# K and V, and pairs of Q units, projected 512 columns at a time in a two-layer trunk

## Chip, cores and metric

The kernel runs on one core of one Trainium2 chip. The metric is the device time of one execution in microseconds (us). The engines of the core are named as the profile names them: PE is TensorE (matmuls; PEld its weight loads), DVE is VectorE, ACT is ScalarE, POOL is GpSimd, SP is SyncE, which mostly issues DMAs. Each engine works through its own instructions in program order and waits on semaphores for the others.

## What is computed

The reference is a trunk of two layers over 512 tokens of width 1024 (fp32). Layer 0 mixes by pooling; layer 1 is sliding-window attention with sink logits over K and V that are computed once, from the stream after layer 0. Each layer ends with a convolutional GLU of width 2816.

```python
D_MODEL = 1024; SEQ = 512; D_FF = 2816
HEAD_DIM = 64; N_Q_HEADS = 16; N_KV_HEADS = 4; WINDOW = 128
# layer 0
x = x + rms_norm(pool_mixer(rms_norm(x, g)), g_post)
x = x + rms_norm(conv_glu_ffn(rms_norm(x, g)), g_post)
# shared K and V
kv = (rms_norm(x, kv_norm_g) @ w_kv).reshape(B, S, 2, 4, 64)
k, v = rope(kv[:, :, 0]), kv[:, :, 1]
# layer 1
q = rope((rms_norm(x, g) @ w_q).reshape(B, S, 16, 64))
m = swa_sink_attention(q, banded(k), banded(v), sinks) @ w_o
x = x + rms_norm(m, g_post)
x = x + rms_norm(conv_glu_ffn(rms_norm(x, g)), g_post)
```

In the attention, a block of 128 queries sees its own block of 128 keys and the one before it, with a causal window of 128; the sink logit of a head enters the maximum and the sum of its softmax only.

## The kernel before

Every large product is computed from fp32 operands that are split into a high and a low fp32r part: high x high, low x high and high x low (`mm3`, lines 318, 319 and 320). So each weight goes through a load from HBM (`raw`), a cast on ACT that makes the high part `wh`, and a subtraction on DVE that makes the low part `wl`. A weight **unit** is 128 x 2048 numbers. `split(i)` makes `wh` and `wl` of unit i in a slot (three slots, or a buffer of its own named in `homes`) and starts the loads of the next two; `ahead` keeps the splits three units in front of the products.

The instructions of PE, ACT, DVE and POOL run in the order in which the program is written; there is no scheduler. In time order the stages are:

- the pooling mixer of layer 0, to about 46 us of the span;
- FFN0's up products. Each of the 22 iterations j of the loop in `first` takes 48 matmuls of 512 columns (`up`), the convolution on ACT and DVE (`act`: lines 535 to 551), sums of the weights for the down product on POOL at even j (`w_sums`), sums of the gated values on POOL at odd j (`g_sums`), and `ahead`. `split1` splits gated values (lines 575, 577, 578);
- FFN0's down products, `pass1` from 289 us and `pass2` to 399 us;
- the projections of K and V, and then the attention with Q's projections, to about 560 us;
- layer 1's FFN, in the same way, to the end.

Six weight units of layer 1 are made ready early: `prepare(i, h)` reads half h of unit i in FFN0's loop, makes its high and low parts, and stores them to DRAM (`ready`). When such a unit is needed, `split` only loads both parts, by DMAs that ACT issues. Units of K, V and Q also get the gain of their normalisation in this place: four casts with a scale on ACT and four operations on DVE (line 174) instead of one and one (line 169). READY holds K, V, two of the four Q units, and two units of FFN1; the 12 halves are prepared at j = 3, 4, 6, 7, 9, 10, 12, 13, 15, 16, 18 and 19:

```python
if l == 0 and j >= 3 and j % 3 != 2 and j < 21:
    k = (j - 3) // 3 * 2 + j % 3
    prepare(READY[k // 2], k % 2)
```

The other two Q units go through `scale` (on POOL, line 183) and `piece` (lines 194 and 198) in the first eight attention steps.

K and V are projected block by block of 128 tokens, 256 columns at a time (`proj`, PSUM tiles `kp` and `vp`): blocks 2 and 3 first, then `to_attention` transposes blocks 0 and 1 of the normalised stream into `xTh_a` and `xTl_a`, with K's own transposes (`k_T`, tile `kt`) between, then blocks 0 and 1. `rotate` applies the rotary embedding (two products on DVE, two sums on POOL), and `kst` is its copy that PE transposes.

The attention has 16 steps, one for each of the four groups of heads g and the four blocks b, in the order of g and then b. Step i issues the scores of its own (g, b), normalises the softmax of step i - 1, transposes the probabilities of step i - 2 (`p_T`, tile `pT`; `PTl` is their low part), multiplies those of step i - 3 with V (`pv`), and projects Q of step i + 3 (`q_proj`, tile `qp`, 24 matmuls of 256 columns). `q_rot`, `q_parts`, `q_low` and `q_T` rotate Q, split it (`qst`) and transpose it (`qt`, then `qT`). The table `todo` spreads Q's and the output projection's weight pieces over the steps. The normalisation is a reciprocal and four products, three on DVE and one on POOL:

```python
for h in range(4):
    eng = nc.gpsimd if h == 3 else nc.vector
    eng.tensor_scalar(Pt[:, h, 0:w], Pt[:, h, 0:w], dn[:, h : h + 1], None, ALU.mult)
```

## Time and profile before

| | |
|---|---|
| three runs | 929.82, 930.46, 934.66 us (median 930.46) |
| the profiled execution | 935.51 us, of which the span is 933.7 us |
| PE, DVE, ACT, POOL busy | 98%, 70%, 50%, 35% of the span |
| mean granted PE clock | 0.99 |
| matmul and other PE instructions | 4702 |

The span runs from the first to the last instruction that the profiler shows. A row of the waits gives who waits at which line for whom, the total in us, how often, and the longest. A row of a timeline gives start and duration in us, engine, line, operation, what it writes and reads with the shape, and how many like it were put together; in brackets stands the idle time before it and what ended that. A row of the groups gives line, engine, operation, tiles, shapes and count, then the busy time in us and the mean in ns, then the idle time in front. Matmuls overlap, so the distance between two starts is their pace, not their duration.

### The profile page before, as it was taken

The page shows a single profiled execution, that of the slowest core. Times are in us where ns is not written, and L with a number is a line of the kernel's source. Part 1 is how long each engine was busy: PE and PEld are TensorE (multiplying, and loading weights), DVE is VectorE, ACT ScalarE, POOL GpSimd, SP SyncE. Part 2 cuts the span into 40 slices and gives each one's busy share as a digit, 9 for nine tenths or more (in the row PEclk, how much of TensorE's full clock was granted, in tenths as well). Part 3 has the DMA queues.
Part 4 walks back from the last instruction along what each step waited for, and adds up shares of the span by engine and source line. Part 5 has one row for each costly group of instructions (what it writes and reads, how often), then busy time and mean ns, then how long its engine had stood idle before and what let it go on. Part 6 is the DMA issues. An engine that isn't in the chain of part 4 may idle for free.

```text
span 933.7 us, 12782 instructions
## 1 busy us (share of the span) xinstructions
PE 912.5 (98%) x4702; PEld 781.0 (84%) x4702; DVE 654.2 (70%) x948; ACT 466.7 (50%) x815; POOL 324.0 (35%) x381
## 2 busy tenths in 40 slices
PE   8999999999999999999999999999999999999996
PEld 7898888888887878799899888988888888888785
DVE  4787867867577777953999836565555565677877
ACT  4734544444445565653688734433334433455562
POOL 1644434444442000234656403244444433410001
PEclk7999999999999999999999999999999999999999
DMA  8263888887884665732112144445554555456642
GB/s 307 91 227 114 312 301 308 257 324 262 295 279 147 218 217 180 277 151 92 47 46 91 49 178 145 149 181 183 202 209 184 205 203 189 159 158 206 219 171 112
DMA packets 45040, 178.49 MB, mean 191 GB/s; under 512 B 5297, under 2 KB 6833, under 8 KB 36658
## 3 DMA queue, kind: packets, MB, share of 16 engines
q1 hardware_dynamic: 43250, 165.10, 50.6%
q10 hardware_dynamic: 1728, 12.58, 3.5%
q8 instruction: 37, 0.61, 0.3%
q14 instruction: 25, 0.20, 0.1%
HBM read 139.91 MB, written 37.75 MB: 190 GB/s over the span
## 4 chain that ended last, share of the span: by engine, by line
PE 79%; DVE 10%; issue 3%; POOL 3%; ACT 3%; DMA 2%; POOLq 0%; SPq 0%; DVEq 0%; ACTq 0%
PE u L319 16%; PE u L320 16%; PE u L318 16%; PE dn L319 5%; PE dn L320 5%; PE dn L318 5%; DVE wl L232 2%; DVE xn_f L303 1%; DVE P L907 1%; PE op L318 1%; PE op L319 1%; PE op L320 1%; PE qp L320 1%; PE qp L318 1%; PE qp L319 1%
## 5 line engine op out<-in xcount | busy, mean ns | idle before, releaser
L319 PE MATMUL u<-xTl_f,wh 128*128 128x512 f32 (+1 forms) x768 | 285.4, 372 | 2.0 <-DVE xTl_f L315 2.0
L318 PE MATMUL u<-xTh_f,wh 128*128 128x512 f32 (+1 forms) x768 | 285.7, 372 | 0.2 <-ACT xTh_f L314 0.2
L320 PE MATMUL u<-xTh_f,wl 128*128 128x512 f32 (+1 forms) x768 | 285.2, 371 | 0.0
L232 DVE TENSOR_TENSOR wl<-raw,wh 128x1024 fp32r<-128x1024 f32 (+1 forms) x158 | 205.8, 1343 | 13.6 <-ACT wh L231 13.3
L319 PEld LDWEIGHTS u<-xTl_f,wh 128*128 128x128 f32 x768 | 144.7, 188 | 27.5 <-DVE xTl_f L315 2.5
L536 DVE SCALAR_TENSOR_TENSOR t<-u,conv,t 128x511 f32<-128x511 f32 x88 | 65.8, 748 | 144.3 <-ACT t L535 144.3
L318 PEld LDWEIGHTS u<-xTh_f,wh 128*128 128x128 f32 x768 | 144.7, 188 | 25.1 <-ACT xTh_f L314 0.5
L320 PEld LDWEIGHTS u<-xTh_f,wl 128*128 128x128 f32 x768 | 144.7, 188 | 25.0
L231 ACT CAST wh<-raw 128x1024 fp32r<-128x1024 f32 (+1 forms) x158 | 156.8, 1040 | 9.2 <-DMA raw<-t 6.4
L535 ACT ACTIVATE t<-u,conv 128x512 f32<-128x512 f32 x88 | 68.2, 776 | 137.3 <-PE u L320 103.2
L556 POOL TENSOR_TENSOR G<-G,G 128x256 f32<-128x256 f32 x22 | 33.3, 1515 | 270.6 <-DVE G L551 270.6
L319 PE MATMUL dn<-wl,gh 128*128 128x512 f32 x276 | 108.0, 391 | 3.1 <-DVE wl L232 3.1
L320 PE MATMUL dn<-wh,gl 128*128 128x512 f32 x276 | 107.6, 390 | 0.1
L318 PE MATMUL dn<-wh,gh 128*128 128x512 f32 x276 | 107.6, 390 | 0.0
L544 ACT ACTIVATE t<-t 128x512 f32<-128x512 f32 x44 | 27.8, 633 | 104.4 <-DVE t L537 104.4
L537 DVE SCALAR_TENSOR_TENSOR t<-u,conv,t 128x510 f32<-128x510 f32 x88 | 65.9, 749 | 3.1
L319 PEld LDWEIGHTS dn<-wl,gh 128*128 128x128 f32 x276 | 51.8, 188 | 15.6 <-DVE wl L232 5.1
L320 PEld LDWEIGHTS dn<-wh,gl 128*128 128x128 f32 x276 | 51.8, 188 | 11.2 <-DVE gl L650 0.6
L318 PEld LDWEIGHTS dn<-wh,gh 128*128 128x128 f32 x276 | 51.8, 188 | 10.8
L252 POOL TENSOR_SCALAR ss_p_f<-ss_p_f 128x1 f32<-128x1 f32 x8 | 3.3, 417 | 159.5 <-ACT dn L250 159.5
L577 ACT CAST gh<-G 128x1024 fp32r<-128x1024 f32 x22 | 23.1, 1051 | 56.4 <-DVE G L575 44.1
L578 DVE TENSOR_TENSOR gl<-G,gh 128x1024 fp32r<-128x1024 f32 x22 | 27.5, 1250 | 26.6 <-ACT gh L577 21.0
(197 smaller groups left out, 1544.9 us busy)
## 6 DMA issues: line engine op xcount, KB each, us to landing
raw<-in_ws_dram SPq DMA_DIRECT2D x49, 1024.0 KB, 5.0
q<-in_ws_dram SPq DMA_DIRECT2D x44, 512.0 KB, 6.4
raw<-t SPq DMA_DIRECT2D x24, 768.0 KB, 5.6
t<-q SPq DMA_DIRECT2D x44, 256.0 KB, 2.9
t<-q SPq DMA_DIRECT2D x22, 512.0 KB, 2.8
raw<-in_ws_dram SPq DMA_DIRECT2D x22, 512.0 KB, 4.4
r<-in_ws_dram SPq DMA_DIRECT2D x12, 512.0 KB, 6.6
hi<-h SPq DMA_DIRECT2D x12, 512.0 KB, 6.4
```

The costliest lines, as they stand in the source:

```text
L231: nc.scalar.copy(hi[:, s], r[:, s])
L232: nc.vector.tensor_tensor(lo[:, s], r[:, s], hi[:, s].bitcast(F32), ALU.subtract)
L318: nc.tensor.matmul(acc, ah, bh, start=first, stop=False)
L319: nc.tensor.matmul(acc, ah, bl, start=False, stop=False)
L320: nc.tensor.matmul(acc, al, bh, start=False, stop=last)
L535: nc.scalar.activation(t, u, AF.Identity, bias=conv_col(l, ch, 3), scale=conv_col(l, ch, 2))
L536: nc.vector.scalar_tensor_tensor(t[:, 1:], u[:, : S - 1], conv_col(l, ch, 1), t[:, 1:], ALU.mult, ALU.add)
L537: nc.vector.scalar_tensor_tensor(t[:, 2:], u[:, : S - 2], conv_col(l, ch, 0), t[:, 2:], ALU.mult, ALU.add)
L544: nc.scalar.activation(tg, tg, AF.Gelu_apprx_tanh)
L556: nc.gpsimd.tensor_tensor(s1, s1, G2[:, p, 2, :], ALU.add)
L577: nc.scalar.copy(h, G1[:, o : o + 1024])
L578: nc.vector.tensor_tensor(lo, G1[:, o : o + 1024], h.bitcast(F32), ALU.subtract)
```

## The change

1. `proj` multiplies 512 columns at a time. K and V are taken together: `prepare` stores the halves of K's and V's units side by side, in 1 KB segments, so that one unit holds K and V for four of the eight k, and the second for the other four. The same is done with Q's units in pairs. A pair's projection takes 4 k from each of two units.
2. READY gets the last two Q units at its end, so all of Q is prepared in FFN0: 16 halves, at all j from 1 to 21 that are no multiple of 4. `scale` and Q's entries of `todo` go; the two units are loaded by ACT's DMAs when needed.
3. The softmax is normalised by one product on DVE over the four heads, with the reciprocal broadcast.
4. The steps run over pairs of groups: (2 pr + i, b) for pr, then b, then i. `q_rot`, `q_parts` and `q_low` work on 512 columns every second step; `q_proj(m, part)` gives one half of a pair's projection per step. The output projection's pieces are spread over steps 4 to 15. Buffers move: `kT` uses the tags `whk` and `wlk`, which a unit of FFN1 takes over; `rA`, `rB` and `st` have fewer and larger buffers; the last `o32` is in `rA`'s. `start1` and `ffn_start(1, ...)` now stand inside the scope of the attention's pool.

```diff
-READY = (U_K, U_V, U_Q, U_Q + 1, U_IN[1], U_IN[1] + 1)
+READY = (U_K, U_V, U_Q, U_Q + 1, U_IN[1], U_IN[1] + 1, U_Q + 2, U_Q + 3)
...
-        nc.sync.dma_start(ready[i][0][:, s], hi.bitcast(F32))
-        nc.sync.dma_start(ready[i][1][:, s], r)
+        if i >= U_IN[1]:
+            o = [t[:, s] for t in ready[i]]
+        else:
+            side = (i - U_K) % 2
+            o = [t.rearrange("p (k s c) -> p k s c", k=4, s=2)[:, :, side, :] for t in ready[i - side + h]]
+            hi, r = (t.rearrange("p (k c) -> p k c", k=4) for t in (hi, r))
+        nc.sync.dma_start(o[0], hi.bitcast(F32))
+        nc.sync.dma_start(o[1], r)
...
-            if l == 0 and j >= 3 and j % 3 != 2 and j < 21:
-                k = (j - 3) // 3 * 2 + j % 3
+            if l == 0 and j % 4:
+                k = j - 1 - j // 4
                 prepare(READY[k // 2], k % 2)
...
+        def proj(u, b, acc, part):
+
+            hi, lo = slots[u + part]
+            for k in range(4):
+                c = slice(k * 512, (k + 1) * 512)
+                kc = part * 4 + k
+                mm3(acc, xTa[0][:, b, kc, :], xTa[1][:, b, kc, :], hi[:, c], lo[:, c], kc == 0, kc == KC - 1)
...
+        def kv_block(b):
+            acc = bank(f"kv{b}")
+            for part in range(2):
+                proj(U_K, b, acc, part)
+            R = rotate(acc[:, 0:256], 4, b, f"k{b}")
+            if b // 2 not in ksts:
+                ksts[b // 2] = pa.tile([P, 2, 4, 2, HD], F32, tag="st", name=f"kst{b // 2}", bufs=2)
+            nc.scalar.copy(ksts[b // 2][:, b % 2], R.unsqueeze(2).to_broadcast([P, 4, 2, HD]))
+            nc.scalar.copy(V[0][:, b, :], acc[:, 256:512])
+            nc.vector.tensor_tensor(V[1][:, b, :], acc[:, 256:512], V[0][:, b, :].bitcast(F32), ALU.subtract)
...
-            for h in range(4):
-                eng = nc.gpsimd if h == 3 else nc.vector
-                eng.tensor_scalar(Pt[:, h, 0:w], Pt[:, h, 0:w], dn[:, h : h + 1], None, ALU.mult)
+            p = Pt[:, :, 0:w]
+            nc.vector.tensor_tensor(p, p, dn.unsqueeze(2).to_broadcast([P, 4, w]), ALU.mult)
...
-        kst[2] = k_block(2)
-        kst[3] = k_block(3)
-        v_block(2)
-        v_block(3)
+        homes[U_Q + 1] = homes[U_O + 1] = (pa, "c")
+        homes[U_IN[1] + 1] = (pa, "k")
+        kv_block(2)
+        kv_block(3)
         to_attention(0)
-        k_T(2, kst[2])
+        k_T(2)
         to_attention(1)
-        k_T(3, kst[3])
+        k_T(3)
         split(U_Q)
...
-        kst[0] = k_block(0)
-        v_block(0)
+        kv_block(0)
         split(U_Q + 1)
-        kst[1] = k_block(1)
-        v_block(1)
+        kv_block(1)
...
-        steps = [(g, b) for g in range(NKV) for b in range(NB)]
+        steps = [(2 * pr + i, b) for pr in range(NKV // 2) for b in range(NB) for i in range(2)]
...
-        todo = [[(U_Q + 2 + i // 4, i % 4)] for i in range(8)]
-        todo += [[(U_O + i // 2, i % 2 * 2), (U_O + i // 2, i % 2 * 2 + 1)] for i in range(8)]
+        todo = {i: [(U_O + (i - 4) // 4, i % 4)] for i in range(4, 12)}
+        todo |= {i: [(U_O + i // 2 - 4, i % 2 * 2), (U_O + i // 2 - 4, i % 2 * 2 + 1)] for i in range(12, 16)}
...
+        q_proj(0, 0)
+        q_proj(0, 1)
         R = q_rot(0)
-        qst[0] = q_parts(*steps[0], R)
-        q_low(qst[0], R)
...
+        q_parts(0, R)
+        q_low(0, R)
+        split(U_Q + 2)
+        split(U_Q + 3)
+        k_T(0)
+        k_T(1)
+        q_proj(1, 0)
+        q_proj(1, 1)
+        qTs[0] = q_T(0)
...
-            if i + 3 < n_s:
-                rot[i + 3] = q_proj(*steps[i + 3])
+            if m + 1 < n_m:
+                q_proj(m + 1, second)
```

Where the engines' order moves, at three places. First DVE's order at the head of FFN0's loop, the end of iteration j = 1, before (t is the convolved value, G the gated product, wl the low part of a unit two ahead, read from raw):

```order
L536 SCALAR_TENSOR_TENSOR t_1_758<-u_1_1_533,conv_145,t_1_758 128x511
L537 SCALAR_TENSOR_TENSOR t_1_758<-u_1_1_533,conv_145,t_1_758 128x510
L551 TENSOR_TENSOR G_0_733<-t_1_758 128x2x256
L232 TENSOR_TENSOR wl_771<-raw_455,wh_770 128x1024 x2
L536 SCALAR_TENSOR_TENSOR t_2_839<-u_2_0_778,conv_145,t_2_839 128x511
```

And the same place of the changed kernel (r and h are the two parts of a prepared half):

```order
L531 SCALAR_TENSOR_TENSOR t_1_762<-u_1_1_537,conv_149,t_1_762 128x510
L545 TENSOR_TENSOR G_0_737<-t_1_762 128x2x256
L175 SCALAR_TENSOR_TENSOR r_0_771<-r_0_771,cst,h_0_772 128x256 x4
L226 TENSOR_TENSOR wl_788<-raw_459,wh_787 128x1024 x2
L530 SCALAR_TENSOR_TENSOR t_2_856<-u_2_0_795,conv_149,t_2_856 128x511
```

Four scaled operations now stand between the gated product and the weight split.

Second, DVE's order at the end of that loop, from the gated product of j = 21 on, before (the first wl is that of the second down unit):

```order
L551 TENSOR_TENSOR G_0_733<-t_21_2383 128x2x256
L232 TENSOR_TENSOR wl_2396<-raw_2241,wh_2395 128x1024 x2
L575 TENSOR_TENSOR G_0_737<-G_0_733,G_0_737 128x256
L578 TENSOR_TENSOR gl_2_2414<-G_0_737,gh_2_2413 128x1024
L232 TENSOR_TENSOR wl_2442<-raw_2325,wh_2441 128x1024 x2
```

And in the changed kernel:

```order
L545 TENSOR_TENSOR G_0_737<-t_21_2426 128x2x256
L175 SCALAR_TENSOR_TENSOR r_1_2435<-r_1_2435,cst,h_1_2436 128x256 x4
L226 TENSOR_TENSOR wl_2452<-raw_2284,wh_2451 128x1024 x2
L569 TENSOR_TENSOR G_0_741<-G_0_737,G_0_741 128x256
L572 TENSOR_TENSOR gl_2_2470<-G_0_741,gh_2_2469 128x1024
L226 TENSOR_TENSOR wl_2498<-raw_2368,wh_2497 128x1024 x2
```

The last prepared half stands in front of the second down unit's wl; before, the last one stood two iterations earlier, and was a plain half.

Third, ACT's order at the turn from K and V to Q, before (from kst of blocks 2 and 3 to the load of Q's second unit, wh_3493 and wl_3494):

```order
L827 COPY kst_3295<-rA_k_3289 128x512
L827 COPY kst_3328<-rA_k_3322 128x512
L841 CAST V_3256<-vp_3330 128x256
L841 CAST V_3256<-vp_3357 128x256
L314 CAST xTh_a<-tr_a_3384 128x512
...
L827 COPY kst_3464<-rA_k_3458 128x512
L841 CAST V_3256<-vp_3466 128x256
L214 DMA wh_3493<-hi_119 128x2048
L214 DMA wl_3494<-lo_120 128x2048
L827 COPY kst_3530<-rA_k_3524 128x512
```

And in the changed kernel, where the load of Q's second unit is wh_3471 and wl_3472:

```order
L826 COPY kst_3351<-rA_k_3345 128x512
L827 CAST V_3312<-kv_3320 128x256
L826 COPY kst_3351<-rA_k_3380 128x512
L827 CAST V_3312<-kv_3355 128x256
L308 CAST xTh_a<-tr_a_3389 128x512
...
L826 COPY kst_3467<-rA_k_3461 128x512
L827 CAST V_3312<-kv_3436 128x256
L214 DMA wh_3471<-hi_119 128x2048
L214 DMA wl_3472<-lo_120 128x2048
L826 COPY kst_3467<-rA_k_3500 128x512
```

The copy of block 3's K now comes third instead of second and reads a product that ends with V's; the load keeps its place behind V's cast of block 0, while its unit is read by the first Q projection's second half instead of by the second group's first.

134 lines of the change are left out of this document (51 added, 83 removed).

## The prediction

> **What bounds the kernel now.** I read the page first, then the waits of TensorE, then the windows by stage.
>
> ```profile
> span 933.7 us, 12782 instructions
> PE 912.5 (98%) x4702; PEld 781.0 (84%) x4702; DVE 654.2 (70%) x948; ACT 466.7 (50%) x815; POOL 324.0 (35%) x381
> ...
> PE 79%; DVE 10%; issue 3%; POOL 3%; ACT 3%; DMA 2%; POOLq 0%; SPq 0%; DVEq 0%; ACTq 0%
> ...
> PE dn L319 <- DVE wl L232: 3.1, 4, 1.3
> ...
> PE pT L915 <- DVE PTl L919: 1.0, 2, 0.6
> PE s L879 <- ACT qT L861: 0.7, 1, 0.7
> ...
> PE qt L858 <- POOL qst L853: 0.2, 1, 0.2
> ...
> 46.00:289.00 243.00, 241.46 (x1159) 203.69 (x1159) 182.16 (x221) 109.99 (x157) 106.49 (x82) 1.00 0.76 264
> ...
> 425.00:560.00 135.00, 133.18 (x917) 122.02 (x916) 101.94 (x286) 89.11 (x262) 63.42 (x112) 1.00 0.20 74
> ```
>
> TensorE (PE) is busy 98% of the span. In the windows (length, then busy PE, weight load, DVE, ACT, POOL, clock, DMA share, GB/s) it idles 1.54 us in FFN0's up products and 1.82 us in the attention stage, at a granted clock of 1.00. So only two things move the time: the number and pace of matmuls, and waits that newly reach PE. Work taken off VectorE (DVE), ScalarE (ACT) or GpSimd (POOL) is worth at most PE's waits for them.
>
> **The pace of the projections.**
>
> ```profile
> 397.76 0.39 PE L320 MATMUL dn<-wh,gl 128*128 128x512 f32 x1
> ...
> 399.35 0.28 PE L318 MATMUL kp<-wh,xTh_a 128*128 128x256 f32 x1
> ...
> 410.86 1.04 PE L311 MATMUL tr_a<-cst,xn_a 128*128 128x128 f32 x8
> ...
> L318 PE MATMUL qp<-wh,xTh_a 128*128 128x256 f32 x128 | 36.5, 285 | 0.0
> ```
>
> Seven 512-column matmuls start between 397.76 and 399.35: 0.227 us each. Between 399.35 and 410.86 stand the 96 of kp2, kp3, vp2 and vp3: 0.120 us each. Two of 256 become one of 512: 2 x 0.120 - 0.227 = 0.013 us. Q has 3 x 128 matmuls, K and V 4 blocks of 48, together 576, so 288 pairs: **-3.7 us**. The operands are the same and PE waits for nothing there, so the ends are near: -3.2 to -4.2 from the rounding of the two pitches.
>
> The Trainium skill, "TensorE: Matmul & The Clock Gate", section "Back-to-back issue gap", gives the warm isolated gap as N/2.4 + 2.5 ns. By that a pair would save 2.5 ns, an estimate of 0.7 us over 288 pairs instead of 3.7; the trace's 256-column pitch of 120 ns lies above the 109 ns of the formula, so the rows count.
>
> **Relief in the attention steps.**
>
> ```profile
> L907 DVE TENSOR_SCALAR P<-P,stat 128x256 f32<-128x256 f32 x36 | 20.0, 610 | 0.4
> L907 POOL TENSOR_SCALAR P<-P,stat 128x256 f32<-128x256 f32 x12 | 12.7, 1057 | 2.8 <-DVE stat L904 2.8
> L198 DVE TENSOR_TENSOR wl<-raw,wh 128x512 fp32r<-128x512 f32 x19 | 13.0, 684 | 0.0
> L183 POOL TENSOR_TENSOR raw<-raw,cst 128x512 f32<-128x512 f32 x8 | 8.3, 1040 | 0.0
> ...
> L578 DVE TENSOR_TENSOR gl<-G,gh 128x1024 fp32r<-128x1024 f32 x22 | 27.5, 1250 | 26.6 <-ACT gh L577 21.0
> ```
>
> A step's normalisation takes 3 x 0.610 = 1.83 us on DVE and 1.06 on POOL beside it. The one product over 128x1024 isn't in the trace. Its nearest row is gl, 1.25 us; the other end is four times 0.610, 2.44. I take 1.25, so DVE wins 0.58 us a step and could lose 0.61. POOL also loses the 8 scalings (8.3 us), and the Q pieces that go take 8 x 0.684 = 5.5 us from DVE and ACT. Of PE's waits these can end pT <- PTl (1.0) and qt <- qst (0.2): **-1.2 us**, between 0 and the window's whole idle, -1.8. The 0.67 of s <- qT is the chain at the first step and stays.
>
> The Trainium skill, "VectorE: DVE Perf Modes", section "Mode 2×_2P", speaks against this edit: a single-source fp32 operation in SBUF gets two elements a cycle, a tensor_tensor one. By its 0.96 GHz that is an estimate of 1.07 us for the one product against 0.40 for three of four heads, so DVE would lose 0.67 a step. The trace shows the three heads at 1.83, not 0.40, so the estimate does not carry.
>
> **FFN0, its head.** Scaled halves are now prepared from j=1, in front of that iteration's weight split.
>
> ```profile
> 79.17 2.90 DVE L232 TENSOR_TENSOR wl<-raw,wh 128x1024 fp32r<-128x1024 f32 x2
> ...
> 96.45 3.12 DVE L174 SCALAR_TENSOR_TENSOR r<-r,cst,h 128x256 fp32r<-128x256 f32 x4
> 99.49 2.31 DVE L232 TENSOR_TENSOR wl<-raw,wh 128x1024 fp32r<-128x1024 f32 x1
> ...
> 109.08 1.67 DVE L174 SCALAR_TENSOR_TENSOR r<-r,cst,h 128x256 fp32r<-128x256 f32 x4
> 110.67 2.36 DVE L232 TENSOR_TENSOR wl<-raw,wh 128x1024 fp32r<-128x1024 f32 x2
> ...
> 82.69 0.39 PE L320 MATMUL u<-xTh_f,wl 128*128 128x512 f32 x1
> ```
>
> At an odd j, POOL's G sums run beside it: the four L174 then take 3.12 and the first half of wl 2.31, so that half ends 101.80 - 96.45 = 5.35 us after the start. At an even j the four take 1.67 and both halves of wl 2.36. At j=1 the half would end at 79.17 + 5.35 = 84.52. PE wants it at 82.69, the third matmul of up(3): **+1.8 us**, 0 if the speed is the even one (79.17 + 1.67 + 1.18 = 82.02). From j=2 to j=18 the stage has the same kind of prepare as before, one more in four iterations; DVE is busy 182.16 of 243 us and the four additional halves add at most 4 x 5.5 = 22, so I cost that at nothing. If three in a row do not fit, that is rival D. SP's queue gets 12 more transfers of 512 KB and loses two loads of 1 MB, and the stores of K, V and Q go out in 1 KB segments; raw is loaded two units ahead of PE, and I take 0, up to +0.5.
>
> **FFN0, its tail.** At j=19 a scaled half stands where a plain one stood, and j=21 gets one where there was none.
>
> ```profile
> 270.39 1.22 DVE L169 TENSOR_TENSOR r<-r,h 128x1024 fp32r<-128x1024 f32 x1
> 271.52 3.44 DVE L232 TENSOR_TENSOR wl<-raw,wh 128x1024 fp32r<-128x1024 f32 x2
> ...
> 277.01 1.23 DVE L578 TENSOR_TENSOR gl<-G,gh 128x1024 fp32r<-128x1024 f32 x1 [1.17 <-POOL q L565]
> ...
> 281.11 0.75 DVE L536 SCALAR_TENSOR_TENSOR t<-u,conv,t 128x511 f32<-128x511 f32 x1 [1.43 <-ACT t L535]
> ...
> 293.41 2.90 DVE L232 TENSOR_TENSOR wl<-raw,wh 128x1024 fp32r<-128x1024 f32 x2
> ...
> 293.57 1.65 POOL L556 TENSOR_TENSOR G<-G,G 128x256 f32<-128x256 f32 x1 [11.44 <-DVE G L551]
> ...
> 294.68 0.50 PE L319 MATMUL dn<-wl,gh 128*128 128x512 f32 x1
> ...
> 300.77 0.50 PE L319 MATMUL dn<-wl,gh 128*128 128x512 f32 x1 [0.35 <-DVE wl L232]
> ```
>
> j=19 grows by 3.12 - 1.22 and by 2 x 2.31 - 3.44: +3.1. The idle places behind it (1.17, 1.43) end with ACT's gh and t, which themselves wait for DVE's work before them, so the delay passes through j=20 and j=21. At 293.41 stands now wl of FFN0's second down unit, and PE takes its first half at 294.68, hardly after it is ready. The new L174 puts 3.12 ahead of it, less some 0.3 since POOL's sums then end while L174 runs: 294.6 + 3.1 + 3.1 - 0.3 = 300.5. PE would wait 5.9 at that place; the 0.5 lost at 300.77 falls away: **+5.4 us**. Bounds: with the even speed, j=19 costs 1.67 + 2.36 - 1.22 - 3.44, nothing, and j=21 1.67, some +1.2; with the slow half of wl too, 301.7, +6.6. This is the largest term. Behind the waiting matmul stands all of pass1, on PE's queue; nothing else is ready for PE.
>
> **The turn to attention.**
>
> ```profile
> 409.30 1.32 ACT L827 COPY kst<-rA_k 128x512 f32<-128x512 f32 x2
> ...
> 411.50 1.07 ACT L314 CAST xTh_a<-tr_a 128x512 fp32r<-128x512 f32 x2
> ...
> 419.43 0.33 ACTq L214 DMA_DIRECT2D wh<-hi  x1
> 419.80 0.44 ACTq L214 DMA_DIRECT2D wl<-lo  x1
> ...
> wl<-lo ACTq DMA_DIRECT2D x6, 1024.0 KB, 7.2
> ...
> L818 DVE TENSOR_TENSOR rA_k<-kp,cos_t 128x256 f32<-128x256 f32 x4 | 1.7, 422 | 3.5 <-PE kp L320 2.7 <-issue 0.8
> L821 POOL TENSOR_TENSOR rA_k<-rA_k,rB_k 128x128 f32<-128x128 f32 x4 | 1.9, 465 | 0.0
> L827 ACT COPY kst<-rA_k 128x512 f32<-128x512 f32 x4 | 2.5, 616 | 6.8 <-POOL rA_k L821 6.7
> ```
>
> K of block 3 now ends with V of block 3: 399.35 + 48 x 0.227 = 410.25 instead of about 405. The rotation (two like 0.422 on DVE, two like 0.465 on POOL) and kst's copy (0.616) follow, 2.4 us and with four hand-overs some 2.7, then V's cast, and only then, in ACT's order, xTh_a. That cast moves from 411.50 to about 413.2, PE has come there 0.6 earlier, and part of it is covered by two transposes: **+1.3 us** (0 to 2.5). Then Q: ACT issues the load of the second unit of Q behind kst and V's cast of block 0 (at 419.43 it was issued as that cast began), so some 2.7 us after that block's products end; it lands 7.2 us later, at 9.9. PE arrives there after 24 x 0.227 + 12 x 0.227 = 8.2: **+1.7 us** (0 to 3). Queued behind are the other half of the first Q pair and all steps. The remaining moves (o32, kT's buffer for an FFN1 unit, one buffer of rA) wait for readers a step or more earlier and I take them as nothing; their cover is 6.5 us of a step.
>
> **The sum.** -3.7 - 1.2 + 1.8 + 5.4 + 1.3 + 1.7 = +5.3 us. The profiled execution took 935.51 (span 933.7 and 1.8 around it), which would become 940.8. It lies 0.5% over the median of the three runs, 930.46; the differences come from PE's pitch and fixed durations, so I add them to the median: **935.8 us**.
>
> **Rivals.**
> A, everything added hides: only -3.7 - 1.2 are left, or -1.8 for the second, 925.0 to 925.6. Against it: ACT's and DVE's order is fixed in the program. For it: PE's waits of before are small.
> B, the other side (not slower): DVE's prepare runs at its even speed, since POOL's sums slide away from it. Place j=1, 19 and 21; price 0 at the head and 1.2 at the tail instead of 1.8 and 5.4; it decides once four L174 take under about 2 us. Sum -1.4: 929.1. For it: 1.67 in the even iterations. Against: at 96.45 POOL and DVE start off the same G.
> C, the turn's two waits are covered (the load lands sooner, PE is late anyway): 935.8 - 3.0 = 932.8.
> D, three prepares in a row overrun DVE in FFN0. An odd iteration holds four operations like L536's 0.75, the 3.12 and two halves of 2.31, 10.7 us, and with G's product over 11 against PE's 48 x 0.227 = 10.9. Each of five groups has two odd ones and could lose 1.0 once its slack is gone: 935.8 + 5 = 940.8. Against it: the even one between has 3 us to spare.
> E, the wider projection brings no pace: 935.8 + 3.7 = 939.5.
>
> **Chances.** Forecast 0.40 (933.5 to 938.5), A 0.12, B 0.22, C 0.14, D 0.08, E 0.04. The range leaves out A and D: 926.5 to 939.5. A measurement of this kernel tells about 0.5% from no change, 4.65 us, so 925.8 and 935.1 are the borders. Faster: A, 0.12. Slower: D, E and two thirds of the forecast's case, 0.40. The same: 0.48.
>
> **What would show it.** Right: PE's wait dn <- wl of about 6 us near 294 to 301, u <- wl near 83 of about 2 us; kv <- xTh_a near 413; qp <- the load near 428; a pitch of 0.227 in qp; a normalise product near 1.25 us and no pT <- PTl. Wrong: L174 of about 1.7 at j=19 and 21, or no wait at pass1's start, which takes the largest term away; a pitch above 0.240, which takes the first.

## The result and the profile after

| | before | changed |
|---|---|---|
| median of 6 runs | 930.56 us (928.89 to 934.66) | 946.34 us (940.27 to 951.39) |
| profiled span | 933.7 us | 945.9 us |

The change made the kernel slower: ratio 1.0158, 95% interval 1.0135 to 1.0182, or 15.8 us. The prediction was 935.8, with a range up to 939.5. From the page of the changed kernel, its span and busy times:

```profile
span 945.9 us, 12132 instructions
...
PE 914.6 (97%) x4414; PEld 768.6 (81%) x4414; DVE 665.3 (70%) x910; ACT 468.0 (49%) x815; POOL 297.2 (31%) x331
```

PE has 288 instructions fewer and is busy 2.1 us longer. Next the waits of PE in the changed kernel (total, times, longest):

```profile
PE dn L313 <- DVE wl L226: 5.7, 4, 3.1
...
PE s L884 <- ACT qT L866: 2.6, 2, 2.0
PE dn L312 <- ACT h L174: 2.0, 1, 2.0
...
PE u L314 <- DVE wl L226: 1.7, 1, 1.7
PE qp L313 <- DMA wl<-lo: 1.6, 1, 1.6
PE qt L863 <- POOL qst L856: 1.4, 1, 1.4
...
PE kt L834 <- ACT kst L826: 0.4, 1, 0.4
```

The waits that were forecast are there: u <- wl at the head of FFN0, dn <- wl at its tail, qp <- the load, and one at the turn, though at kt <- kst and not at kv <- xTh_a. Not forecast are dn <- h, s <- qT (one of two; the other stood before) and qt <- qst. But the new waits sum to some 11 us, and the loss is larger. To see where, PE's own rows are used as marks: the first instruction of each stage, first in the kernel before,

```profile
44.45 0.47 PE L318 MATMUL u<-xTh_f,wh 128*128 128x256 f32 x1
...
288.95 0.39 PE L318 MATMUL dn<-wh,gh 128*128 128x512 f32 x1
...
424.99 0.28 PE L318 MATMUL qp<-wh,xTh_a 128*128 128x256 f32 x1
...
435.76 0.33 PE L879 MATMUL s<-kT,qT 128*128 128x128 f32 x1 [0.67 <-ACT qT L861]
...
513.80 0.28 PE L879 MATMUL s<-kT,qT 128*128 128x256 f32 x1
...
517.45 0.39 PE L318 MATMUL op<-wh,o_parts 128*128 128x512 f32 x1
...
574.77 0.28 PE L318 MATMUL u<-xTh_f,wh 128*128 128x256 f32 x1
```

and then in the changed one:

```profile
41.86 0.47 PE L312 MATMUL u<-xTh_f,wh 128*128 128x256 f32 x1
...
288.37 0.39 PE L312 MATMUL dn<-wh,gh 128*128 128x512 f32 x1
...
407.31 0.39 PE L312 MATMUL kv<-wh,xTh_a 128*128 128x512 f32 x1
...
418.69 0.27 PE L305 MATMUL tr_a<-cst,xn_a 128*128 128x128 f32 x1
...
433.49 0.39 PE L312 MATMUL qp<-wh,xTh_a 128*128 128x512 f32 x1
...
448.42 0.33 PE L884 MATMUL s<-kT_whk,qT 128*128 128x128 f32 x1 [0.68 <-ACT qT L866]
...
515.49 0.28 PE L884 MATMUL s<-kT_whk,qT 128*128 128x256 f32 x1
...
528.32 0.46 PE L312 MATMUL op<-wh,o_parts 128*128 128x512 f32 x1
...
586.57 0.28 PE L312 MATMUL u<-xTh_f,wh 128*128 128x256 f32 x1
```

The row at 513.80 before and at 515.49 after is the first one behind the last projection of Q. The table gives the time between the marks and, in the last two columns, what is left over PE's own pace: the number of matmuls in the stage by 0.227 us (512 columns), 0.120 (256) or 0.110 (128; eight transposes take 410.86 to 411.73 in the kernel before). This rest is called the **excess** from here on.

| stage | before | after | excess before | excess after |
|---|---|---|---|---|
| FFN0's up products | 244.5 | 246.5 | 1.8 | 3.8 |
| FFN0's down products | 110.4 | 118.9 | 3.8 | 12.3 |
| K, V of blocks 2 and 3 | 11.5 | 11.4 | 0.0 | 0.5 |
| transposes, K, V of blocks 0 and 1 | 14.1 | 14.8 | 0.0 | 1.3 |
| first Q to first scores | 10.8 | 14.9 | 0.8 | 2.7 |
| scores to last projection of Q | 78.0 | 67.1 | 2.8 | 0.6 |
| from there to the output projection | 3.7 | 12.8 | 0.0 | 6.2 |
| to FFN1's first product | 57.3 | 58.3 | 0.4 | 0.2 |

The times grow by 14.4 us, the excess by 18, and the pace gives back the 3.7 that were forecast. Ahead of the first up product the programs do the same work, and that mark lies anywhere from 37.9 to 44.5 us in the profiles of this study: at 37.9 to 39.5 where the granted clock stayed at full speed, and at 41.8 to 44.5 where it stood at half for 6.8 or 10.2 us from about 12 or 13 us on. So stages are compared from there on.

The clock makes up the difference between waits and excess. The windows of the changed kernel (length, busy PE, PEld, DVE, ACT, POOL, then the granted clock), in steps of 3.41 us on whose borders that clock changes (the last section shows how they were found):

```profile
292.91:296.32 3.41, 1.35 (x5) 0.89 (x6) 2.03 (x3) 3.41 (x7) 0.00 (x0) 1.00 0.17 70
296.32:299.74 3.42, 1.25 (x4) 0.38 (x2) 3.42 (x6) 1.34 (x2) 2.48 (x3) 0.50 0.59 180
299.74:303.15 3.41, 2.49 (x6) 2.01 (x7) 2.34 (x3) 0.98 (x2) 0.00 (x0) 0.50 0.51 172
303.15:306.56 3.41, 3.41 (x10) 2.63 (x9) 3.31 (x3) 1.97 (x3) 0.00 (x0) 0.50 0.96 257
518.19:521.60 3.41, 1.45 (x10) 1.00 (x8) 2.91 (x11) 2.66 (x9) 2.26 (x5) 1.00 0.57 243
521.60:525.02 3.42, 2.07 (x11) 1.89 (x10) 3.42 (x5) 3.20 (x8) 3.17 (x2) 0.50 0.03 7
525.02:528.43 3.41, 3.41 (x12) 2.83 (x11) 2.91 (x10) 3.08 (x11) 1.59 (x3) 0.50 0.01 2
```

In two places PE works at half its clock behind a wait: from 296.32 to 306.56 and from 521.60 to 528.43 us. A product of 512 columns then starts every 0.427 us instead of 0.227 (301.68 to 306.37), so 47% of PE's busy time there is lost: by this estimate some 3.3 us of 7.15 at the first place and 2.6 of 5.48 at the second. Before the change the clock stood at 1.00 in the windows of up products and attention, and in that of the down products, too:

```profile
289.00:399.00 110.00, 107.52 (x478) 87.70 (x477) 88.70 (x101) 64.26 (x85) 11.96 (x18) 1.00 0.62 215
```

How the tail came about, first on DVE (two fences), then on PE (rows of the timeline of the changed kernel):

```profile
269.80 3.12 DVE L175 SCALAR_TENSOR_TENSOR r<-r,cst,h 128x256 fp32r<-128x256 f32 x4
...
296.39 3.08 DVE L175 SCALAR_TENSOR_TENSOR r<-r,cst,h 128x256 fp32r<-128x256 f32 x4
299.40 2.35 DVE L226 TENSOR_TENSOR wl<-raw,wh 128x1024 fp32r<-128x1024 f32 x2
```

```profile
295.00 0.75 DVE L531 SCALAR_TENSOR_TENSOR t<-u,conv,t 128x510 f32<-128x510 f32 x1
```

```profile
295.90 0.47 PE L312 MATMUL dn<-wh,gh 128*128 128x512 f32 x1 [2.04 <-ACT h L174]
...
300.66 0.79 PE L313 MATMUL dn<-wl,gh 128*128 128x512 f32 x1 [3.09 <-DVE wl L226]
```

L175 takes the slow 3.1 us both times, and the first half of wl is ready at 300.6. The forecast said 300.5. The wait comes in two parts. The second, 3.09 us, is the one that was forecast, for wl behind the half of j = 21. The first, 2.04 us, is put down to ACT's h, but DVE's last convolution operation of j = 21 (L531) ends at the same moment. The run e1_tail, which prepares nothing at j = 21, decides between them: the same wait stands there at the same place, 7.53 us behind the first down product.

```profile
296.48 0.65 PE L312 MATMUL dn<-wh,gh 128*128 128x512 f32 x1 [2.02 <-DVE t L531]
```

So the first part is the delay of j = 19's half, handed on through the convolutions, as the forecast had it; it reaches PE at a place of its own.

The second place is step 12, the first one without a projection of Q:

```profile
520.55 0.38 PE L884 MATMUL s<-kT_whk,qT 128*128 128x256 f32 x1 [1.96 <-ACT qT L866]
...
523.14 1.12 PE L863 MATMUL qt<-cst,qst 128*128 128x128 f32 x4 [1.35 <-POOL qst L856]
```

```profile
518.94 0.51 ACT L896 ACTIVATE P<-P,stat 128x256 f32<-128x256 f32 x1 [1.21 <-DVE stat L893]
...
519.94 0.56 ACT L866 CAST qT<-qt 128x512 fp32r<-128x512 f32 x1
...
521.10 1.98 POOL L856 TENSOR_TENSOR qst<-rA_q,qst 128x512 fp32r<-128x512 f32 x1 [0.61 <-ACT qst L852]
```

PE is through with step 12 within 3 us of 515.49. The scores of step 13 need qT, which ACT casts behind two exponentials of step 12, which wait for DVE's maxima, which stand behind Q's rotation. Then the transposes of Q for step 14 wait for POOL's low part of 512 columns (1.98 us).

### The profile page after: what moved, and what is told of

It reads as the page before. It is cut to its first block, busy times and chain, and to the rows that moved or that the text cites. A ratio compares the mean times of both kernels' runs of the same rounds, so it can differ in the third digit from the quotient of the medians.

```text
span 945.9 us, 12132 instructions
## 1 busy us (share of the span) xinstructions
PE 914.6 (97%) x4414; PEld 768.6 (81%) x4414; DVE 665.3 (70%) x910; ACT 468.0 (49%) x815; POOL 297.2 (31%) x331
## 4 chain that ended last, share of the span: by engine, by line
PE 76%; DVE 10%; DMA 4%; issue 3%; ACT 3%; POOL 3%; ACTq 0%; DVEq 0%; SPq 0%; POOLq 0%
PE u L314 15%; PE u L313 15%; PE u L312 15%; PE dn L313 5%; PE dn L312 5%; PE dn L314 5%; DVE wl L226 3%; DMA wl<-lo 2%; DVE xn_f L297 1%; PE op L312 1%; PE op L314 1%; PE op L313 1%; PE qp L313 1%; PE pT L919 1%; PE qp L314 1%
## 5 line engine op out<-in xcount | busy, mean ns | idle before, releaser
L226 DVE TENSOR_TENSOR wl<-raw,wh 128x1024 fp32r<-128x1024 f32 (+1 forms) x158 | 211.7, 1380 | 13.7 <-ACT wh L225 13.5
L550 POOL TENSOR_TENSOR G<-G,G 128x256 f32<-128x256 f32 x22 | 30.5, 1384 | 258.7 <-DVE G L545 258.7
L531 DVE SCALAR_TENSOR_TENSOR t<-u,conv,t 128x510 f32<-128x510 f32 x88 | 65.9, 749 | 3.1
L313 PEld LDWEIGHTS dn<-wl,gh 128*128 128x128 f32 x276 | 52.5, 190 | 18.2 <-DVE wl L226 7.5
L312 PEld LDWEIGHTS dn<-wh,gh 128*128 128x128 f32 x276 | 52.6, 190 | 14.4 <-ACT h L174 2.4
```

Of the source, the lines that this page charges most:

```text
L226: nc.vector.tensor_tensor(lo[:, s], r[:, s], hi[:, s].bitcast(F32), ALU.subtract)
L312: nc.tensor.matmul(acc, ah, bh, start=first, stop=False)
L313: nc.tensor.matmul(acc, ah, bl, start=False, stop=False)
L531: nc.vector.scalar_tensor_tensor(t[:, 2:], u[:, : S - 2], conv_col(l, ch, 0), t[:, 2:], ALU.mult, ALU.add)
L550: nc.gpsimd.tensor_tensor(s1, s1, G2[:, p, 2, :], ALU.add)
```

## The experiments

All ratios are against the kernel before, run on the same chip, with the 95% interval. Kernels that start from the changed one are compared with it by their stages: its own six runs lie 11 us apart, and the runs of e3_fill and e13_order 9 us, so a difference of a few us between two of these medians says little.

| run | from | edit | median us | ratio |
|---|---|---|---|---|
| e1_tail | changed | half of j = 21 at j = 8 | 942.0 | 1.0117 (1.0089 to 1.0145) |
| e2_sched | changed | nothing prepared at 1 and 21, plain halves last | 935.35 | 1.0038 (1.002 to 1.0057) |
| e3_fill | changed | output projection in step 12 | 943.49 | 1.0126 (1.0073 to 1.0179) |
| e4_load | changed | Q's second unit loaded earlier | 941.95 | 1.0116 (1.0089 to 1.0142) |
| e6_hold | changed | 28 empty matmuls in the tail's wait | 945.41 | 1.0161 (1.0136 to 1.0187) |
| e11_hold12 | changed | 12 of them | 943.44 | 1.0137 (1.0106 to 1.0168) |
| e13_order | changed | steps of block 0 at 12 and 13 | 947.6 | 1.0165 (1.0126 to 1.0203) |
| e5_norm | before | the one-product softmax alone | 931.4 | 1.001 (0.9996 to 1.0024) |
| e10_noqp | before | last projection in step 11 | 929.93 | 0.9996 (0.998 to 1.0013) |
| e12_ahead | before | all projections one step earlier | 934.59 | 1.003 (1.0012 to 1.0047) |
| e14_qearly | before | all Q units prepared in FFN0 | 929.09 | 0.9976 (0.9961 to 0.9992) |
| e7_all | changed | e2, e3 and e4 together | 928.38 | 0.9984 (0.9965 to 1.0002) |
| e8_oldnorm | e7_all | softmax as before | 928.01 | 0.9968 (0.9952 to 0.9984) |
| e9_todo | e7_all | fewer pieces in step 12 | 929.38 | 0.9988 (0.9974 to 1.0002) |
| e15_todo_old | e9_todo | softmax as before | 929.53 | 0.998 (0.9964 to 0.9997) |

### The tail of FFN0: order or transfers

```diff
-            if l == 0 and j % 4:
-                k = j - 1 - j // 4
+            if l == 0 and j in (1, 2, 3, 5, 6, 7, 8, 9, 10, 11, 13, 14, 15, 17, 18, 19):
+                k = (1, 2, 3, 5, 6, 7, 8, 9, 10, 11, 13, 14, 15, 17, 18, 19).index(j)
```

> The changed kernel with the prepared half of j = 21 moved to j = 8; the order of the halves is the same, and all 16 remain. Theory (the order on VectorE and ScalarE makes the wait at the start of the down products, and TensorE's clock drops because of that wait): only j = 19's 3.1 us of delay are left, so the wait of 5.5 us becomes 2.0 to 3.1, the clock stays at 1.00 there, and the time falls by 5 to 6.5 us from 946.3, to about 940.5. Rival (the loads and stores of more prepared halves hold up the weights' loads): the transfers are as many as before, so the wait stays above 4 us and the time within 2 us of 946.3. Second rival (any wait of 2 to 3 us there halves the clock): a fall of only 2.5 to 3.5 us, to about 943.5.

The down products took 114.5 us instead of 118.9, and the median fell by 4.3 us. What is left is the wait of 2.0 us (dn <- t) that j = 19's half causes, and a clock of 0.65 and 0.50 from 296 to 300 us. So DVE's order is the cause, and not the transfers, which were as many; of the theory's size, the part on the clock was wrong: even this wait was followed by half a clock, for a shorter time. The result lies between the theory and the second rival.

```diff
-READY = (U_K, U_V, U_Q, U_Q + 1, U_IN[1], U_IN[1] + 1, U_Q + 2, U_Q + 3)
+READY = (U_K, U_V, U_Q, U_Q + 1, U_Q + 2, U_Q + 3, U_IN[1], U_IN[1] + 1)
...
+            if l == 0 and j in (2, 3, 4, 5, 6, 7, 8, 9, 10, 12, 13, 14, 15, 16, 18, 19):
...
```

> The changed kernel with the halves prepared at j = 2 to 10, 12 to 16, 18 and 19, all Q units first and the two plain FFN1 units last, so that nothing is prepared at j = 1 and 21 and the halves at 18 and 19 are plain as in the kernel before. Theory: head and tail of FFN0 are as before the change; the waits u <- wl (1.7) and dn <- wl, h (5.5) and the half clock near 300 us go, 10.5 us in all, to about 936. Rival (three and more prepares in a row overrun VectorE): up's matmuls wait for wl between j = 2 and 11, 2 to 8 us, and the time is 938 to 944.

935.35 us. The excess of the up products is 1.8 and that of the down products 3.8 us, both as before the change: all of the 10.5 us that head and tail cost are gone, with the same 16 halves and the same transfers. Nine prepares in a row do not overrun DVE. The load of Q's second unit landed later in this profile; its wait:

```profile
PE qp L313 <- DMA wl<-lo: 2.3, 1, 2.3
```

The granted clock was 0.69 from 424 to 428 us. A wait of 2.3 us cost 2.3 and a slower clock behind it, an excess of 5.0 in that stage against 2.7 with a wait of 1.6 and the clock at 1.00.

### The tail's clock

```diff
             for q in of:
                 make(q, p)
+            if l == 0 and p == 0:
+                for n in range(28):
+                    nc.tensor.matmul(X[7][n % 2][0:64], zero, g_parts[l, 1, 0][0][:, 0:512], start=False, stop=False)
             ahead(U_D1[l] + p)
```

> The changed kernel with 28 added matmuls (512 columns, a zero weight, so that they add nothing) behind the first down unit's products, where TensorE waits 2.0 and 3.1 us; 28 x 0.227 = 6.4 us. They do nothing for the result. Theory (the clock drops to 0.50 because TensorE idles there, and the drop costs some 3 us on top of the wait): the clock stays at 1.00 near 296 to 306 us, the excess of the down products over the nominal pace falls from 12.3 to 9 to 10 us, and the time by 2 to 3.5 us, to about 943.5. Rival (the clock drops there for another reason, or the waits' lengths are all there is to it): no fall, or a rise of 1 us.

The row of the empty matmuls on PE, which ran after the first part of the wait:

```profile
293.39 7.44 PE L617 MATMUL dn<-gh,zero 128*64 128x512 f32 x28
```

They took until 300.66 and so longer than the wait: the next real product started 16.2 us into the stage, 3.9 later than without them. From there to K's first product it was 104.0 us (300.66 to 404.69) instead of 106.6 (300.66 to 407.31): the clock was full again at 295.10, 10.7 us into the stage instead of 18.2, and stayed. The expected fall did not come, for 28 were too many; but behind them the stage was 2.6 us shorter. So the run was repeated with 12:

> As the run with 28 added matmuls of zero weight, with 12 of them. There the 28 took 7.27 us and ended 3.9 us later than the wait they replaced, and everything behind them up to K's first product took 104.0 us instead of 106.6. Theory (the clock recovers after a few us of unbroken work and stays): the 12 end at about the time at which the wait ends in the changed kernel, and the down products take 116 to 117 us instead of 118.9, 2 to 3 us less, with a clock of 1.00 from about 3 us behind the first wait on. Rival (the gain in that run was chance): 118.5 to 119.5.

117.0 us for the down products instead of 118.9, with the clock at 1.00 again. The same data arrived at the same time; only PE did not idle for the second part. In the four profiles with no edit there the stage took 118.3 to 120.3 us. By these two runs 1.9 to 2.6 us of the tail's 8.5 fall to the half clock; counted in the changed kernel's windows above it is some 3.3.

### The hole at step 12

```diff
-        fill_late = {n_s - 3: [(0, 0), (0, 1)], n_s - 2: [(1, 0)], n_s + 2: [(3, 0), (3, 1)]}
+        fill_late = {n_s - 4: [(0, 0)], n_s - 3: [(0, 1)], n_s - 2: [(1, 0)], n_s + 2: [(3, 0), (3, 1)]}
```

> The changed kernel with one of the two output projections of step 13 (block 0, first half, 12 matmuls, 2.7 us) issued in step 12, the first step without a projection of Q. Theory (step 12 has lost TensorE's work that covered its chain, 24 matmuls that the kernel before issued there): the waits s <- qT (1.96) and qt <- qst (1.35) near 520 us shrink to under 1 us together, the clock stays at 1.00 there, and the time falls by 4.5 to 6 us, to about 941. Rival (VectorE's chain with the rotation of 512 columns and the longer product is too long by itself, whatever TensorE does): the wait moves to step 13, and the time falls by under 2 us.

The excess behind the last projection fell from 6.2 to 0.0, and 2.4 of it came back in the steps after it (0.2 to 2.6): qt <- qst still waits 0.9 at step 13, which now has 12 matmuls less, and pT <- PTl 0.6. Net 3.9 us (2.9 by the medians): less than the theory's 4.5 to 6, and well over the rival's 2. Three more runs asked what had opened the hole.

```diff
-            if i + 3 < n_s:
-                rot[i + 3] = q_proj(*steps[i + 3])
+            for k in {n_s - 5: (i + 3, i + 4), n_s - 4: ()}.get(i, (i + 3,)):
+                if k < n_s:
+                    rot[k] = q_proj(*steps[k])
```

> The kernel before with its last projection of Q (step 15's, 24 matmuls of 256 columns, 2.9 us) issued in step 11 instead of step 12, so that step 12 has none, as in the changed kernel. Theory (what opened the hole at step 12 is the missing cover of TensorE): TensorE waits for qT or qst at the start of step 13, 1.5 to 4 us, the clock may drop, and the time rises by 2 to 6 us. Rival (the hole needs the change's own longer operations, the rotation of 512 columns and the product over four heads): waits under 1 us, a rise of under 1 us.

No wait and no change. The theory in this form fell: an empty step 12 alone does nothing, if step 11 holds two projections. That the other engines catch up in step 11 is a likely reason, and was not shown. Another difference seemed to be left: in the kernel before, step 12 is one of block 0, with half the softmax.

```diff
+        BS = (0, 1, 2, 3, 1, 2, 0, 3)
...
-            pr, b = divmod(m, NB)
+            pr, b = m // NB, BS[m]
...
-        steps = [(2 * pr + i, b) for pr in range(NKV // 2) for b in range(NB) for i in range(2)]
+        steps = [(2 * (m // NB) + i, BS[m]) for m in range(2 * NB) for i in range(2)]
```

> The changed kernel with the blocks of the second pair of groups in the order 1, 2, 0, 3 instead of 0, 1, 2, 3, so that steps 12 and 13 are those of block 0, whose softmax has 128 keys instead of 256; in the kernel before, step 12 was a step of block 0, too. Theory (step 12 opened a hole since the new order of the steps put a full step where TensorE has no projection left): TensorE's excess between the last projection of Q and the output projection falls from 6.2 to under 2.5 us, the time to about 942. Rival (the missing cover alone, or the rotation of 512 columns, makes it): it stays above 5 us.

The excess went from 6.2 to 5.2 only (s <- qT 1.5, qt <- qst 1.6), and five other profiles without this edit have 5.1 to 6.2. This theory fell, too: a light step does not close the hole.

```diff
+        rot[3] = q_proj(*steps[3])
         qTs[0] = q_T(*steps[0], qst[0])
...
-            if i + 3 < n_s:
-                rot[i + 3] = q_proj(*steps[i + 3])
+            if i + 4 < n_s:
+                rot[i + 4] = q_proj(*steps[i + 4])
```

> The kernel before with four projections of Q ahead of the steps instead of three, so that each step projects for the fourth step after it and step 12 has none, without a double one in step 11; step 12 is a step of block 0 with 128 keys. Theory as in the run of the order (a full step without cover is needed): TensorE's excess in steps 12 and 13 stays under 1.5 us. Rival (the missing projection alone makes the hole): 2.5 us or more, and the time rises by 2 to 5 us.

The rival held. The excess there is 2.7 us. Two rows of its PE, whose clock stayed at 1.00:

```profile
509.00 0.39 PE L879 MATMUL s<-kT,qT 128*128 128x256 f32 x1 [1.51 <-DVE stat L904]
...
511.72 0.76 PE L915 MATMUL pT<-cst,P 128*128 128x128 f32 x5 [0.48 <-POOL P L907]
```

So a projection taken out of the steps and put ahead of them is what opens the hole, in the old kernel with its old operations as well. In the changed one the same loss costs 3.3 us in waits, with qT behind a rotation of 512 columns and qst's low part of 512, and the clock drops there and adds some 2.6.

### The load of Q's second unit

```diff
+        split(U_Q + 1)
         nc.scalar.activation(tab, nsink[:, 0:1], AF.Exp)
         kv_block(0)
-        split(U_Q + 1)
         kv_block(1)
```

> The changed kernel with the load of Q's second unit issued by ScalarE before the products of K and V of block 0 instead of behind V's cast of that block. Theory (the load is issued too late by ScalarE's order): qp <- wl (1.6 us) goes, the time falls by 1 to 2 us, to about 945. Rival (the transfer is late because of the queue's or the memory's rate): the wait stays above 1 us.

qp <- wl is gone, and the excess of the stage is 0.8 instead of 2.7 (2.0 to 5.0 in the seven profiles that keep the load's place). ScalarE's order was the cause. The median fell by 4.4, more than the 1.9 of this profile; that this wait is at times followed by a lower clock, as in e2_sched, may be the rest.

### The softmax, and what relieved the steps

```diff
-            for h in range(4):
-                eng = nc.gpsimd if h == 3 else nc.vector
-                eng.tensor_scalar(Pt[:, h, 0:w], Pt[:, h, 0:w], dn[:, h : h + 1], None, ALU.mult)
+            p = Pt[:, :, 0:w]
+            nc.vector.tensor_tensor(p, p, dn.unsqueeze(2).to_broadcast([P, 4, w]), ALU.mult)
```

> The kernel before with one edit of the change alone, the softmax normalised in one product over four heads on VectorE. Theory (the product costs VectorE 1.2 to 1.25 us for 1.83 and frees GpSimd): TensorE's stalls between the first scores and the last projection of Q, 2.8 us over the nominal pace in the profile of before, shrink by 1 to 2 us, and the time moves by -1 to -2 us, hardly to be told from 931. Rival (the product is slowed by GpSimd's sharing to 2 us or more in most steps): no gain there or a loss of up to 1.5 us.

The rival held: the excess in the steps rose from 2.8 to 4.5 us. Two groups and a wait of this kernel show why, with the group of POOL in the kernel before the change behind them:

```profile
L906 DVE TENSOR_TENSOR P<-P,stat 128x1024 f32<-128x1024 f32 x12 | 17.1, 1426 | 0.4
L853 POOL TENSOR_TENSOR qst<-rA_q,qst 128x256 fp32r<-128x256 f32 x14 | 19.6, 1401 | 3.7 <-ACT qst L849 3.7
```

```profile
PE qt L858 <- POOL qst L853: 2.2, 4, 1.0
```

```profile
L853 POOL TENSOR_TENSOR qst<-rA_q,qst 128x256 fp32r<-128x256 f32 x16 | 12.2, 765 | 4.8 <-ACT qst L849 4.2 <-DVE P L907 0.5
```

The product itself is shorter on DVE than the three it replaces (1.43 for 1.83 us). But POOL's low part of Q now takes 1.40 us instead of 0.77, and PE's transposes wait for that (qt <- qst 2.2 instead of 0.2). Before, it ran beside VectorE's tensor_scalar products and took 0.73 to 0.88 us; in e5_norm it takes 0.73 to 0.74 where no such product runs, and 1.00 to 1.72 beside the tensor_tensor product and the weight piece behind it. The Trainium skill, "GPSIMD Engine Reference", section "8. Key points", says that GpSimd shares its SBUF interfaces with VectorE, with contention from VectorE instructions that read two SBUF inputs; the near doubling of POOL's operation beside a tensor_tensor agrees.

So the softmax is not what took the steps' excess from 2.8 to 0.6 in the changed kernel. One part of the change was put into the kernel before by itself:

```diff
-        todo = [[(U_Q + 2 + i // 4, i % 4)] for i in range(8)]
+        todo = [[] for i in range(8)]
...
-        scale(*todo[0][0])
+        split(U_Q + 2)
+        split(U_Q + 3)
...
-            if i + 1 < n_s and todo[i + 1][0][0] < U_O:
-                scale(*todo[i + 1][0])
...
```

with READY and the halves as in e2_sched.

> The kernel before with one part of the change alone: all Q units are prepared in FFN0 (halves at j = 2 to 10, 12 to 16, 18 and 19, plain ones last), so the scalings on GpSimd and Q's pieces leave the attention steps; the projections stay at 256 columns, the steps' order and the softmax as before. Theory (it is this relief that ends TensorE's stalls in the steps): the excess from the first scores to the last projection of Q falls from 2.8 to under 1.2 us, the time by 1 to 2.5 us. Rival (it needs the rotation of 512 columns every second step): it stays above 2 us and the time at 931.

The excess in the steps fell to -0.1, which is none: the three paces are rounded. The early preparation of Q alone gives all of the relief, 2.9 us in the profile, and neither head nor tail of FFN0 pays for it with this schedule. By the runs' times it is 0.24% faster than before.

### The mends together

> The changed kernel with three mends together: the prepared halves at j = 2 to 10, 12 to 16, 18 and 19 with the plain ones last, one output projection from step 13 in step 12, and the load of Q's second unit issued before the products of K and V of block 0. Theory (the terms add): 946.3 - 9.6 - 3.9 - 2 to 4 = 929 to 931, the same as before the change or 0.2% under it. Rival (the waits take each other's place): above 933.

928.38 us: the terms add, and the 15.8 us become a gain of 2, which the interval (0.9965 to 1.0002) does not tell from no change. The old softmax in the same kernel:

> The kernel with all three mends and with the softmax normalised as before the change (three products on VectorE, one on GpSimd). Theory (the one product brings no gain: it raised TensorE's excess in the steps from 2.8 to 4.5 us in the kernel before): the steps' excess stays at 0.5 to 1.5 us, and the time is within 1 us of the 928.4 of the mended kernel. Rival (the product is what removed the steps' stalls in the changed kernel): the excess rises above 2 us and the time by 1.5 to 3 us.

928.01 us, the lowest of the study, 0.32% under the kernel before. The steps' excess is the same with both (0.7): once the steps have slack, the product neither helps nor hurts. Its expectation's theory holds.

```diff
-        todo = {i: [(U_O + (i - 4) // 4, i % 4)] for i in range(4, 12)}
-        todo |= {i: [(U_O + i // 2 - 4, i % 2 * 2), (U_O + i // 2 - 4, i % 2 * 2 + 1)] for i in range(12, 16)}
+        todo = {i: [(U_O + (i - 4) // 4, i % 4)] for i in range(4, 11)}
+        late = [(U_O + 1 + k // 4, k % 4) for k in range(3, 12)]
+        todo |= {11: late[:2], 12: late[2:3], 13: late[3:5], 14: late[5:7], 15: late[7:]}
```

> The kernel with all three mends, where the output projection's weight pieces start one step earlier per unit (two at step 11, one at step 12 and none of it on GpSimd there), so that step 12 holds one piece instead of two. Theory (what is left of the hole, 2.6 us of excess in steps 12 to 15, hangs on GpSimd's piece beside the low part of Q and VectorE's piece that it slows to 1.76 us): qt <- qst (0.9 us) goes and the excess falls to under 1.5 us, the time by about 1 us to 927.5. Rival (the chain of the full steps alone): no change in the excess.

The theory fell. The excess rose from 2.6 to 3.4 us, and qt <- qst from 0.9 to 1.4, perhaps since the second piece of step 11 delays the engines before step 12. Taking a piece out of step 12 does not close the rest of the hole; that the chain of full steps keeps it open was argued only.

> The same as the run before it with the softmax normalised as before the change. Theory (the product neither helps nor hurts once the steps have slack): within 1 us of that run. Rival (the mix of three and one slows the end of the steps, where GpSimd has no piece): over 1 us slower.

929.53 us, the same as the run before it, with an excess there of 4.1 instead of 3.4.

## Why the prediction was wrong

It forecast +5.3 us and 15.8 came, 14.4 of them between the marks. Step by step:

- **Pace of the projections, -3.7: right.** A 512-column matmul starts every 0.227 us, and the sum of the paces is 3.7 lower. Where nothing waits, in e4_load, K and V of blocks 2 and 3 take 10.89 us instead of 11.51: 0.013 us a pair, as forecast.
- **FFN0's head, +1.8: right**, 2.0 in the stage; PE waits for wl at 82 us, by the path described.
- **FFN0's tail, +5.4: right in its mechanism, wrong in its size.** wl's first half came 12.2 us behind the first down product for a forecast of 11.6 (300.5 less 288.95; that both read 300.5 or 300.6 on their spans is chance), and the waits are 2.0 and 3.1 us in place of one of 5.9. But the term priced a long wait of PE at its length. The half clock behind it adds some 3.3 us, of which e6_hold and e11_hold12 took 2.6 and 1.9 away, so the stage lost 8.5. The Trainium skill, "TensorE: Matmul & The Clock Gate", section "What's actually happening", states that the clock falls to half after an idle window of about 3.4 us; the prediction weighed another section of that page and not this one, while it forecast a wait of 5.9. Here less idle time was enough: 2.06 of the 3.41 us from 292.91 on.
- **The turn, +1.3 and +1.7: right in size.** K and V of blocks 0 and 1 lose 1.3 us, and the first Q 1.9 more than before. But PE's wait at the turn is the 0.4 of kt <- kst, one place ahead of the xTh_a that was named. K and V of blocks 2 and 3 lose 0.5 that were not forecast, with a wait of 0.2 for the load of their second unit.
- **Relief in the steps, -1.2: -2.2 came, beyond its bound of -1.8, and one of its two causes was wrong.** The prediction gave it to the one-product softmax and to the scalings and pieces of Q that go. The product alone raises the excess (e5_norm), and Q's early preparation alone ends it (e14_qearly).
- **"The remaining moves [...] I take them as nothing": the step that failed.** It looked at the buffers that move and not at where the projections of Q end. With four halves ahead of the steps, the last one stands in step 11, and step 12 is left without the work that covers ACT's, DVE's and POOL's chain. That cost 6.2 us, 3.3 in waits and some 2.6 in clock; work put into step 12 (e3_fill) takes 3.9 of it away, and in the kernel before, the missing projection alone makes 2.7 (e12_ahead). The prediction treated the steps as one stage with one relief, and the order of PE at their end was not read.

Stage by stage the marks give -3.7 + 2.0 + 8.5 + 1.8 + 1.9 - 2.2 + 6.2 - 0.2 = 14.3 of the 14.4 us. The forecast lacked 3.1 of the tail and the 6.2 of the hole; its other errors, 1.0 too little relief and 0.9 too little at head and turn, nearly cancel, which is luck. The rivals did not come: VectorE did not run at its even speed (3.1 for four L175, not 1.7), and three prepares in a row, even nine, did not overrun it. The sum of rival B is wrong: with 0 and 1.2 in the place of 1.8 and 5.4 it is -0.7 and not -1.4, so 929.8 us and not 929.1; it stays on the same side of both borders.

## What to carry to other kernels

A wait of TensorE of some 2 us or more is to be priced above its length, for the clock that can fall behind it: look for the places where a change makes one, above all at a stage's ends. When work that covers a chain is moved ahead in a pipeline, look at where it now runs out: there the cover is missing by just as much. And an operation that is shorter on one engine can be longer for the chain, if it falls beside another engine's operation on the path.

## What the runs showed of the hardware

A wait of one length was followed by half a clock in one profile and by a full one in another: the load of Q's second unit waited 2.04 us in e3_fill and 2.01 in e13_order, at the same place of the program. What differs is where the wait fell. In the traces' record the granted clock changes only at multiples of 3.41 us from each other: in the changed kernel at 296.32, 306.56, 521.60 and 528.43, which lie 3, 63 and 2 times 3.413 us apart. The time between is taken here in windows of 3.41 us on that grid. Each wait on PE stands with the window that ends during it or behind it, and with the next one; first e3_fill, then e13_order:

```profile
439.88 0.50 PE L313 MATMUL qp<-wl,xTh_a 128*128 128x512 f32 x1 [2.04 <-DMA wl<-lo]
```

```profile
436.14:439.56 3.42, 1.70 (x8) 1.08 (x6) 0.42 (x1) 0.89 (x2) 0.62 (x2) 1.00 0.70 275
439.56:442.97 3.41, 3.09 (x16) 2.58 (x17) 0.20 (x1) 0.00 (x0) 0.00 (x0) 1.00 0.00 0
```

```profile
439.47 0.50 PE L313 MATMUL qp<-wl,xTh_a 128*128 128x512 f32 x1 [2.01 <-DMA wl<-lo]
```

```profile
436.48:439.89 3.41, 1.40 (x7) 0.85 (x6) 0.42 (x1) 0.82 (x2) 0.00 (x0) 1.00 0.43 180
439.89:443.30 3.41, 3.41 (x10) 2.63 (x9) 0.00 (x0) 0.00 (x0) 0.00 (x0) 0.50 0.00 0
```

In e3_fill a border cuts the wait, so PE idled 1.7 us in one window and 0.3 in the next; in e13_order all 2.0 lie in one window, and the next ran at half clock. The stage's excess was 3.2 us with the first and 4.7 with the second.

All 17 profiles say the same, between FFN0's first up product and PE's last one. PE idled 1.77 us or more in 16 windows at full clock, and half a clock followed every time; in the other 4329 such windows it idled 1.71 us or less, and half a clock followed once, behind 1.62 (in e4_load, at the end of the down products). Behind a window at half clock the full clock came back where PE had idled 0.66 us or less in it, and not where it had idled 0.92 or more. So in these runs the limit lies near half a window, and a wait of 2 us costs its length alone or a window at half clock more, by where it falls. Such a window costs up to 3.41 x (1 - 0.227 / 0.427) = 1.6 us, an estimate from the two paces of 512 columns. Filling the gap with work ends the half clock sooner (10.7 instead of 18.2 us into the down products, in e6_hold).

The spread of the runs goes with the clock: the changed kernel's six runs go from 940.27 us, at a mean granted clock of 0.995, to 951.39, at 0.983. Which of their windows were slow is not known, for one of the six alone has a profile.

POOL's subtraction over 128x256 took 0.73 to 0.88 us beside VectorE's tensor_scalar products and 1.00 to 1.72 beside its tensor_tensor ones.
